# Two halves of the rows per partition, and an output in two pieces, in a row-wise Poisson loss kernel

## The chip, the core and the metric

The kernel runs on one core of one Trainium2 chip. The metric is the device time of one execution in microseconds (us), as a median over several runs. The profile is of one further execution, which has its own time and, within it, a span: the time from the first to the last instruction that the profiler recorded.

The core has a vector engine (DVE), a scalar engine (ACT), a general engine (POOL, GpSimd), a matrix engine (unused here) and a sync engine (SP). SP issues all of this kernel's memory transfers (DMAs), which run on 16 DMA engines between the chip's memory (HBM) and the on-chip memory of 128 partitions (SBUF). Engines wait for each other and for DMAs by semaphores; a finished DMA adds 16 to its semaphore.

## What is computed

```
batch, dim = 1024, 4096                       # float32
log_input = np.random.randn(batch, dim)
target    = np.random.randint(0, 10, (batch, dim)).astype(np.float32)

loss = np.exp(log_input) - target * log_input
return np.mean(loss, axis=-1).astype(np.float32)     # 1024 numbers
```

Two inputs of 16.8 MB each are read once, and 4 KB are written.

## The kernel before

Each of the 128 partitions takes 8 rows of the inputs, called rows 0 to 7 of the partition; a row is d = 4096 elements, 16 KB. In the kernel before, partition p has the rows 8p to 8p+7 of the batch, which lie behind one another in memory: 128 KB of each input per partition. Below, x is log_input and t is target.

**Loads (L62 to L69, issued at L123 to L133).** Thirteen loads alternate between x and t, all on SP, in this order: rows 0 to 3 of x, then of t (64 KB a partition, 8 MB each); rows 4 and 5 of x, then of t (32 KB a partition, 4 MB each); row 6 of x, then of t (16 KB a partition); and row 7 in the seven pieces of `TAIL` (in 32nds of a row: x 24, t 12, t 12, x 6, t 5, x 2, t 3). Every load covers all 128 partitions. The first four are moved ahead of the program's first barrier by `before_first_barrier`. Rows 6 and 7 reuse the buffers of rows 0 to 3 (`x_big`, `t_big`; see `place`), so the load of row 6 waits until the first exponential and the first product are done, and the loads of row 7 until four of each are (L124 to L127). Rows 4 and 5 have the buffers `x_mid` and `t_mid`. Each load has its own semaphore, `landed[i]`; the last of them, `landed[-1]`, belongs to the last piece of x, and the last load of all, the last piece of t, counts on `last_ready`.

**ACT (L149 to L166).** For each row of x, or piece of row 7, one activation computes the exponential, throws the values away (`e_dump`) and keeps the sum (`accum_out`). For rows 0 to 6 a small second activation (`join`, L139 to L147) later adds the row's sum of exponentials and DVE's sum of negated products, scales by 1/d, writes the result to column `row` of `all_loss` and raises `join_done`.

**DVE (L169 to L202).** For each row of t, or piece of row 7, one instruction multiplies t and x, and keeps the negated sum. The last one (L193) also multiplies the partial sums of row 7, which lie right behind the data, with a stretch of -1, and so closes row 7: it writes column 7 of `all_loss` and raises `loss_done`. It waits for the last load and for the last exponential.

**Output (L205 to L212).** SP waits for all seven joins and for `loss_done`, and writes `all_loss`, 128 partitions of 8 numbers, to the output in one DMA; then it clears the semaphores and waits for that DMA.

What decides where a row of the batch goes is three views of the inputs and the output (L57 to L59), and with them the distance in memory between the pieces that neighbouring partitions read in one load.

Of the kernel before, what the change touches and what calls it, by code (L numbers as in the profile page):

```python
# [30 lines left out]
def kernel(tc, log_input, target, out):  # L31
# [11 lines left out]

    nc = tc.nc
    tc.close()
    tc.compile()  # L48

    P = nc.NUM_PARTITIONS  # L50
    n, d = log_input.shape
    nb = n // P
# [1 line left out]
    inv_d = 1.0 / d  # L54
    last_row = nb - 1

    x_v = log_input.rearrange("(p b) d -> p (b d)", b=nb)  # L57
    t_v = target.rearrange("(p b) d -> p (b d)", b=nb)
    out_v = out.rearrange("(p b) -> p b", b=nb)  # L59


    loads = []  # L62
# [30 lines left out]
    def place(what, lo, w):  # L93
        row = lo // d
        if 4 <= row < 6:
            return mid[what][:, lo - 4 * d : lo - 4 * d + w]
        if row >= 6:
            lo -= (6 if row == 6 else 4) * d
        return big[what][:, lo : lo + w]
# [5 lines left out]
    all_loss = nc.alloc_sbuf_tensor("all_loss", [P, nb], F32).ap()  # L105
# [4 lines left out]
    landed = [nc.alloc_semaphore(f"landed{i}") for i in range(len(loads) - 1)]  # L110
# [5 lines left out]
    join_done = nc.alloc_semaphore("join_done")  # L116
    ones_done = nc.alloc_semaphore("ones_done")
    loss_done = nc.alloc_semaphore("loss_done")
    out_done = nc.alloc_semaphore("out_done")
# [3 lines left out]
    for i, (what, lo, w) in enumerate(loads):  # L123
        if what == "x" and lo in (6 * d, 7 * d):  # L124
            free = 1 if lo == 6 * d else 4
            nc.sync.wait_ge(exp_done, free)
            nc.sync.wait_ge(prod_done, free)  # L127
        src = x_v if what == "x" else t_v
        dma = nc.sync.dma_start(out=place(what, lo, w), in_=src[:, lo : lo + w])  # L129
        dma.then_inc(landed[i] if i < len(loads) - 1 else last_ready, 16)  # L130
        if lo < 6 * d:
            early.append(dma.ins)
# [16 lines left out]
    for k, (lo, w, i) in enumerate(x_work):  # L149
# [3 lines left out]
        elif col == 0 and row == 1:  # L153
            nc.scalar.wait_ge(exp_done, k)
        nc.scalar.activation(  # L155
            out=e_dump[:, col : col + w],
            in_=place("x", lo, w),
# [11 lines left out]
    for j, (lo, w, i) in enumerate(t_work):  # L169
# [4 lines left out]
        if j < n_t - 1:  # L174
            nc.vector.tensor_tensor_reduce(  # L175
                out=place("t", lo, w),
# [12 lines left out]
        else:  # L189
# [4 lines left out]
                out=place("t", lo, w + n_parts),  # L194
# [7 lines left out]
            ).wait_op(last_ready, 18, "sem-ge").then_inc(loss_done, 1)  # L202


    nc.sync.wait_ge(join_done, last_row)  # L205
    nc.sync.dma_start(out=out_v, in_=all_loss).wait_op(loss_done, 1, "sem-ge").then_inc(
        out_done, 16
    )
    used = landed + [last_ready, exp_done, prod_done, join_done, ones_done, loss_done]
    nc.sync.sem_clear(range(used[0].num, out_done.num))  # L210
    assert all(used[0].num <= s.num < out_done.num for s in used)
    nc.sync.wait_ge(out_done, 16).then_inc(out_done, -16)  # L212


# [28 lines left out]
```

## Time and profile before

| what | value |
|---|---|
| median of 7 runs | 84.04 us (83.95 to 84.72) |
| the profiled execution, its whole time | 84.15 us |
| its span | 82.8 us |
| DMA | 33.56 MB in 2016 packets, mean 405 GB/s |
| DVE busy | 35.6 us, 22 instructions |
| ACT busy | 33.2 us, 35 instructions |
| last piece of x landed | 80.20 us into the span |
| output's DMA issued | 81.36 us into the span |

A packet is one row of a load on one DMA engine (one partition's piece), or one of the 16 small writes that report a DMA's end: 14 DMAs of 128 rows and 16 reports make the 2016. The share of the DMA is the mean busy share of the 16 engines. In the chain of waits the profile follows the work that ended last back to what released each step; "issue" is time in which nothing shown was waited for, and SPq is an issue on SP. L129 and so on are lines of the kernel.

### The profile page before, as it was taken

What the parts mean: (1) busy time and instruction counts of PE and PEld (TensorE: products, weight loads), DVE (VectorE), ACT (ScalarE), POOL (GpSimd) and SP (SyncE); (2) the same over time, 40 slices, a digit from 0 to 9 for tenths busy, and PEclk for the clock granted to TensorE, in tenths of its full rate; (3) what the DMA queues carried; (4) which work ended last, traced back from release to release, by engine and by line L of the source; (5) the groups of instructions that cost most, each with busy time, mean ns of one, the idle gap of its engine ahead of it and who ended that gap; (6) DMA issues with size and microseconds to landing.
All of it is one profiled execution on the core that took longest, in us unless ns stands there. A gap on an engine that the chain in (4) does not pass through costs nothing.

```text
span 82.8 us, 131 instructions
## 1 busy us (share of the span) xinstructions
DVE 35.6 (43%) x22; ACT 33.2 (40%) x35; POOL 0.3 (0%) x5
## 2 busy tenths in 40 slices
DVE  0000000000000000000199999999369995994992
ACT  0500000000499910000000998979792496019360
POOL 0000000000000000000000000000000000000000
DMA  9389999958999995899599799899899999999950
GB/s 507 158 348 507 507 507 507 443 222 348 507 507 507 507 443 222 348 507 507 253 507 475 301 491 491 364 412 507 348 404 404 467 396 433 392 421 427 408 205 2
DMA packets 2016, 33.56 MB, mean 405 GB/s; under 512 B 352, under 2 KB 608, under 8 KB 1120
## 3 DMA queue, kind: packets, MB, share of 16 engines
q1 hardware_dynamic: 2016, 33.56, 95.6%
HBM read 33.55 MB, written 0.00 MB: 405 GB/s over the span
## 4 chain that ended last, share of the span: by engine, by line
DMA 72%; DVE 18%; issue 4%; SPq 3%; ACT 1%
DMA t_big<-in_target_dram 49%; DMA x_big<-in_log_input_dram 23%; DVE t_big L175 17%; SPq L129 3%; DVE t_big L193 1%; ACT e_dump L155 1%; DVE parts L175 0%; SPq L127 0%; DVE all_loss L193 0%
## 5 line engine op out<-in xcount | busy, mean ns | idle before, releaser
L175 DVE CUSTOM_DVE_ANT_0 t_big<-t_big,x_big 128x4096 f32<-128x4096 f32 (+2 forms) x8 | 26.2, 3307 | 43.6 <-DMA t_big<-in_target_dram 43.4
L155 ACT ACTIVATE e_dump<-x_big 128x4096 f32<-128x4096 f32 (+3 forms) x8 | 21.8, 2729 | 24.1 <-DMA x_big<-in_log_input_dram 24.0
L175 DVE CUSTOM_DVE_ANT_0 t_mid<-t_mid,x_mid 128x4096 f32<-128x4096 f32 x2 | 8.8, 4424 | 2.1 <-DMA t_mid<-in_target_dram 2.1
L141 ACT ACTIVATE join_dump<-parts 128x2 f32<-128x2 f32 x7 | 1.4, 204 | 20.4 <-DVE parts L175 20.2
L155 ACT ACTIVATE e_dump<-x_mid 128x4096 f32<-128x4096 f32 x2 | 7.1, 3568 | 0.0
L155 ACT ACT_TABLE_LOAD x1 | 1.3, 1283 | 3.0 <-PEq L48 3.0
L155 ACT ACTIVATION_READ_ACCUMULATOR e_dump<-x_big 128x1 f32 x8 | 1.5, 186 | 0.0
L141 ACT ACTIVATION_READ_ACCUMULATOR join_dump<-parts 128x1 f32 x7 | 1.3, 187 | 0.0
L193 DVE CUSTOM_DVE_ANT_0 t_big<-t_big,x_big 128x390 f32<-128x390 f32 x1 | 0.6, 566 | 0.1
L175 DVE DVE_READ_ACCUMULATOR2_ANT parts<- 128x1 f32 x7 | 0.6, 84 | 0.0
L155 ACT ACTIVATION_READ_ACCUMULATOR e_dump<-x_mid 128x1 f32 x2 | 0.4, 186 | 0.0
L175 DVE DVE_READ_ACCUMULATOR2_ANT t_big<- 128x1 f32 x3 | 0.2, 82 | 0.0
L136 POOL MEMSET x_big<- 128x6 f32 x1 | 0.1, 104 | 2.6 <-POOLq L48 2.6
L227 POOL MEMSET const-uint8-127<- 128x1 uint8 x1 | 0.1, 103 | 0.0
L227 POOL MEMSET const-bfloat16-1.0<- 128x1 bf16 x1 | 0.1, 102 | 0.0
L227 POOL MEMSET const-float32-0.0<- 128x1 f32 x1 | 0.1, 99 | 0.2 <-issue 0.2
L227 POOL MEMSET const-float32-1.0<- 128x1 f32 x1 | 0.1, 99 | 0.0
L193 DVE DVE_READ_ACCUMULATOR2_ANT all_loss<- 128x1 f32 x1 | 0.1, 84 | 0.0
## 6 DMA issues: line engine op xcount, KB each, us to landing
x_mid<-in_log_input_dram SPq DMA_DIRECT2D x1, 4096.0 KB, 50.0
t_mid<-in_target_dram SPq DMA_DIRECT2D x1, 4096.0 KB, 59.3
x_big<-in_log_input_dram SPq DMA_DIRECT2D x1, 2048.0 KB, 20.0
t_big<-in_target_dram SPq DMA_DIRECT2D x1, 2048.0 KB, 24.5
x_big<-in_log_input_dram SPq DMA_DIRECT2D x1, 1536.0 KB, 15.5
t_big<-in_target_dram SPq DMA_DIRECT2D x2, 768.0 KB, 17.7
x_big<-in_log_input_dram SPq DMA_DIRECT2D x1, 384.0 KB, 18.9
t_big<-in_target_dram SPq DMA_DIRECT2D x1, 320.0 KB, 19.2
```

Source lines behind the costliest of these rows:

```text
L129: dma = nc.sync.dma_start(out=place(what, lo, w), in_=src[:, lo : lo + w])
L136: nc.gpsimd.memset(big["x"][:, 4 * d : 4 * d + n_parts], -1.0).then_inc(ones_done, 1)
L141: nc.scalar.activation(out=join_dump[:, 2 * row : 2 * row + 2], in_=parts[:, 2 * row : 2 * row + 2], func=ACT_F.Copy, scale=inv_d, accum_o ...
L155: nc.scalar.activation(out=e_dump[:, col : col + w], in_=place("x", lo, w), func=ACT_F.Exp, bias=0.0, scale=1.0, accum_out=parts[:, 2 * ro ...
L175: nc.vector.tensor_tensor_reduce(out=place("t", lo, w), in0=place("t", lo, w), in1=place("x", lo, w), scale=-1.0, scalar=0.0, op0=ALU.mult ...
L193: nc.vector.tensor_tensor_reduce(out=place("t", lo, w + n_parts), in0=place("t", lo, w + n_parts), in1=place("x", lo, w + n_parts), scale= ...
L227: nc = _bacc.Bacc("TRN2", target_bir_lowering=False, num_devices=1)
```

## The change

The batch is cut into two halves of 512 rows. Partition p now has the rows 4p to 4p+3 of the first half as its rows 0 to 3, and the rows 4p to 4p+3 of the second half (512+4p and on) as its rows 4 to 7. The list of loads, their sizes, their order and waits stay; the pieces of neighbouring partitions in one load are 64 KB apart in memory instead of 128 KB. The first load of x and the first load of t each read 8 MB that lie without a gap; rows 4 and 5 together, row 6, and the pieces of row 7 are read with gaps, in stretches of 32 KB, 16 KB and less, 64 KB apart.

The output belongs to two separate places for each partition, and is written by two DMAs of 128 partitions of 4 numbers. The first is issued once the last piece of x has landed and the joins of rows 0 to 3 are done, the second when the rest is done. The wait at the end is for both.

```diff
-    x_v = log_input.rearrange("(p b) d -> p (b d)", b=nb)
-    t_v = target.rearrange("(p b) d -> p (b d)", b=nb)
-    out_v = out.rearrange("(p b) -> p b", b=nb)
+    x_v = log_input.rearrange("(h p b) d -> p h (b d)", h=2, p=P)
+    t_v = target.rearrange("(h p b) d -> p h (b d)", h=2, p=P)
+    out_v = out.rearrange("(h p b) -> p h b", h=2, p=P)
+    half = nb // 2
...
-        dma = nc.sync.dma_start(out=place(what, lo, w), in_=src[:, lo : lo + w])
+        h, at_lo = divmod(lo, half * d)
+        dma = nc.sync.dma_start(out=place(what, lo, w), in_=src[:, h, at_lo : at_lo + w])
...
+    nc.sync.wait_ge(landed[-1], 16)
+    nc.sync.dma_start(out=out_v[:, 0, :], in_=all_loss[:, :half]).wait_op(
+        join_done, half, "sem-ge"
+    ).then_inc(out_done, 16)
     nc.sync.wait_ge(join_done, last_row)
-    nc.sync.dma_start(out=out_v, in_=all_loss).wait_op(loss_done, 1, "sem-ge").then_inc(
-        out_done, 16
-    )
+    nc.sync.dma_start(out=out_v[:, 1, :], in_=all_loss[:, half:]).wait_op(
+        loss_done, 1, "sem-ge"
+    ).then_inc(out_done, 16)
...
-    nc.sync.wait_ge(out_done, 16).then_inc(out_done, -16)
+    nc.sync.wait_ge(out_done, 32).then_inc(out_done, -32)
```

In the changed kernel the loads are issued at L132, the first output at L209 and the second at L213.

## The prediction

> **What bounds the kernel now.** I read the page's queue part and the shares of the chain first, because they name the resource that is short.
>
> ```profile
> DVE 35.6 (43%) x22; ACT 33.2 (40%) x35; POOL 0.3 (0%) x5
> ...
> q1 hardware_dynamic: 2016, 33.56, 95.6%
> ...
> DMA 72%; DVE 18%; issue 4%; SPq 3%; ACT 1%
> ```
>
> The one DMA queue is busy for 95.6% of sixteen engines' span, and no compute engine is busy for half of it. The 18% that the chain gives to DVE is work done while the transfers run on (the chain follows a buffer that L127 waits for, at 58.7 us, and DMA is busy all that while).
>
> Then I asked for the DMA share and rate by window (last two columns), to see whether the transfers run at a ceiling of the engines or lose time between packets or in memory.
>
> ```profile
> 1.00:1.50 0.50, 0.00 (x0) 0.00 (x0) 0.00 (x0) 1.00 6.15 2097
> ...
> 6.00:7.00 1.00, 0.00 (x0) 0.00 (x0) 0.00 (x0) 1.00 2.42 1049
> 41.00:59.00 18.00, 17.47 (x8) 12.01 (x15) 0.00 (x0) 1.00 1.01 433
> 59.00:73.00 14.00, 11.22 (x5) 7.87 (x8) 0.00 (x0) 1.00 0.96 408
> 73.00:80.50 7.50, 6.18 (x7) 4.37 (x7) 0.00 (x0) 1.00 0.91 366
> ...
> 82.00:82.50 0.50, 0.00 (x0) 0.00 (x0) 0.00 (x0) 1.00 0.15 8
> ```
>
> A packet counts in the window in which it starts, so a short window can show a share over 1. 2097 GB/s for 0.5 us is 1.05 MB, sixteen packets of 64 KB, one for each engine; their share, 6.15 x 0.5 us, is 3.07 us a packet. From 6 to 7 us another sixteen start and take 2.42 us each. So the first packets are 0.65 us longer than the later ones, and a later one moves at 65,536 B / 2.42 us = 27.1 GB/s, or 433 GB/s for sixteen. From 41 to 59 us the measured rate is that same 433 with a share of 1.01: no engine idles. At 433 GB/s the 33.55 MB need 77.5 us; they take some 79.0 (first packets from about 1.1 us, the last data at about 80.2). The missing 1.5 us are the 0.65 of the first packets and the small packets of the tail (366 GB/s after 73 us).
>
> Last I read the end of the chain, for what follows the last byte, and SP's timeline, because the new instruction stands on SP.
>
> ```profile
> 61.14 19.06 DMA x_big<-in_log_input_dram
> 80.20 0.02 issue
> 80.22 0.52 ACT e_dump L155 x2
> 80.74 0.02 issue
> 80.76 0.57 DVE t_big L193
> 81.33 0.01 DVE all_loss L193
> ```
>
> ```profile
> 58.74 0.33 SPq L129 DMA_DIRECT2D x_big<-in_log_input_dram  x1
> 59.11 0.98 SPq L129 DMA_DIRECT2D t_big<-in_target_dram  x2
> 60.13 0.44 SPq L129 DMA_DIRECT2D x_big<-in_log_input_dram  x1
> 60.61 0.48 SPq L129 DMA_DIRECT2D t_big<-in_target_dram  x1
> 61.14 0.46 SPq L129 DMA_DIRECT2D x_big<-in_log_input_dram  x1
> 61.64 0.44 SPq L129 DMA_DIRECT2D t_big<-in_target_dram  x1
> 81.36 0.35 SPq L206 DMA_DIRECT2D out_dram<-all_loss  x1
> ```
>
> ```profile
> out_dram<-all_loss SPq DMA_DIRECT2D x1, 4.0 KB, 1.4
> ```
>
> After the last piece of x lands (80.20) come the last exponential, the closing DVE reduction, the output's issue at 81.36, and its landing 1.4 us later (82.76), which is the end of the 82.8 us span. The profiled execution took 84.15, so 1.35 lie around the span; the median of the seven runs is 84.04, 0.11 below. I sum against 84.15 and take the 0.11 off at the end.
>
> **The change, part by part.** *Where the loads read from.* All thirteen loads keep 128 partitions, bytes per partition, order and waits; only the distance in memory from one partition's piece to the next falls from 128 KB to 64 KB, so that the two 8 MB loads read one unbroken stretch and the others read half or less of a stretch with gaps. Packets are no larger. In the steady part a packet takes what sixteen busy engines give it (2.42 us, 433 GB/s at full share), whether it belongs to the 8 MB loads (64 KB packets) or to the 4 MB loads between 41 and 59 us (32 KB pieces, 128 KB apart, half of memory skipped): skipping costs nothing there. So I price the steady part at 0. The cover for that is the engines' own rate: were it memory that set the 2.42 us, each 1% of packet time would be worth 0.79 us.
>
> The only place where the trace leaves room for the address is the first sixteen packets, 0.65 us over the rest. Either that is the cost of starting (nothing is in flight before), which no layout changes, or sixteen engines that start together at equal distances meet in the same part of memory, which another distance may cure or make worse. Bounds: -0.65, the excess gone, and +0.65, as much again. The trace has no second cold start to decide by. I take 0: the loads that begin later, at other addresses and with the queue full, show no such excess (the 41 to 59 us window holds the starts of 4 MB loads and is at the ceiling), which fits a cost of starting.
>
> The Trainium skill has a rule here, in "DMA: Bandwidth & Descriptors", section "Latency and other measured facts": HBM-to-HBM copies whose rows lie a large power of two apart slow down, 207 GB/s at 512 KiB and 103 at 4 MiB against 214 in full, and tensors should be laid out contiguously. By that rule the change goes the good way, but its mildest entry loses 3%, already at four times our distance, and the 433 GB/s windows leave nothing of the kind at 128 KB; by the rule at its mildest the sum would be 3% of 79 us lower, some 81.7, an estimate that the rows contradict.
>
> *The early output.* One DMA of 128 rows of 16 B (columns 0 to 3 of all_loss) is issued after landed[-1], the semaphore of the last x piece, and after four joins. The joins of rows 0 to 3 are over by 60 us, so landed[-1] decides: 80.20. SP then issues from about 80.25 to 80.6 (0.35, the row at 81.36), and the data land 1.4 us after the issue's start, about 81.65. Queued behind it on SP are the wait for seven joins (the last at 77.5 us) and the final output, which needs loss_done at 81.34. So SP is free 0.7 us before it is wanted. No load stands behind it: L129's last issue is at 61.64. Nobody but the final wait looks for this output's landing, 1.1 us before the final one. Cost on the path: 0. What hides it is the 1.14 us of exponential and reduction; if that cover were gone, the price is one more issue, 0.44 to 0.48 by the rows that follow one another.
>
> The Trainium skill speaks against such a split, in "DMA: Bandwidth & Descriptors", section "Rules for kernel authors": many small transfers should be coalesced into one, since below 64 KB nearly all is overhead. Put on the path in full, the row's 1.4 us would give 84.04 + 1.4 = 85.4; the trace puts it beside the last exponential and reduction.
>
> *The final output.* 2 KB instead of 4 KB, still 128 rows. In the window from 82.0 to 82.5 us the output's 128 packets and 16 completion writes share 0.15 x 0.5 us x 16 = 1.2 us, 8.3 ns each, nine on an engine: 0.075 us in all. Half the bytes can save at most half of that, 0.04; the rows give no sign that a 16 B packet is quicker than a 32 B one, so 0. Its issue is 0.35 after long idleness and 0.43 to 0.49 right behind another; here some 0.75 us of idleness lie between, nearer to the first: 0, with +0.14 as the bound. Four instead of two rows of results now share 64 B of memory; if that slowed the writes, the nearest row is again the 0.075 us, so +0.08 when doubled. The final wait for 32 instead of 16 is the same instruction: 0.
>
> *The compute engines.* Same instructions, sizes and order on DVE, ACT and GpSimd; only which rows of the inputs they work on differs. 0.
>
> Sum: 84.15 + 0 = 84.15 for a profiled execution, or 84.04 for the median; I write 84.05. The forecast's own bounds: -0.04 for the smaller output, +0.22 for the issue and the small writes, and 0.1 either way, from the six runs that lie between 83.95 and 84.10: 83.9 to 84.35.
>
> **The rivals.** *A: the start was a collision, and the denser layout cures it.* For: sixteen packets at 3.07 against 2.42 us, and all loads gain a shorter distance. Against: the excess looks like a cold start. Price: up to -0.65, so 83.4; it decides from 0.42 on.
>
> *B: the denser layout collides.* Sixteen engines in step at half the distance lose what the first packets lost once more, at the start or where a load begins. For: the same excess. Against: full rate in the windows. Price +0.65: 84.7, slower; it decides when the extra packet time passes 0.42 us on the slowest engine, 17% of one 64 KB packet.
>
> *C: the early output gets into the way of the final one.* If SP or the queue takes longer than 1.1 us over the first (its landing takes 1.4), the second starts late: +0.44 to +0.48, so 84.5. Against: six issues in a row, 0.5 us apart at most.
>
> *D: the change doesn't do what it says.* If the loads were cut into other packets, their count would change. The instructions have the same shapes; I expect 2016 + 128 + 16 = 2160 packets. Under D the time is 84.04 too.
>
> **How the numbers follow.** Differences below about 0.5% (0.42 us) can't be told from none here. Forecast, with D: 0.73. A: 0.13. B: 0.08. C: 0.06. Thus faster 0.13, same 0.73, slower 0.14. The range takes in the forecast's own 83.9 to 84.35, the weaker half of A and C, and most of the way to B: 83.55 to 84.6.
>
> **What would show it.** Right: the 41 to 59 us rate stays at 433; the first sixteen packets stay near 3.07 us; the last x piece lands at 80.0 to 80.4; L209 issues right there and L213 about 1.1 us later, landing after 1.4. A shows as a shorter first share (under 5.5), B as a longer one or a lower rate in a window, C as L213 issued more than 0.1 us after loss_done. A steady rate over 433 would prove wrong that the engines set the pace, and with it the forecast.

## The result: slower by 0.9%, and the profile after

The changed kernel takes 84.86 us in the median of 12 runs (84.51 to 85.3), the kernel before 84.04 in 31 runs. The ratio is 1.0094, 95% interval 1.0072 to 1.0116: slower by 0.6 to 1.0 us, clear of the 0.5% named above. The single runs are spread over 0.8 us; of the 31 of before, 27 lie between 83.83 and 84.19. The profiled execution, 84.67 us with a span of 83.3, is one of the shorter ones; against that of before (84.15, 82.8) it is 0.5 us longer.

The page first: packets and busy share of the DMA queue of the changed kernel, and the line of the output DMAs (count, KB each, median us from issue to landing).

```profile
q1 hardware_dynamic: 2160, 33.56, 95.2%
```

```profile
out_dram<-all_loss SPq DMA_DIRECT2D x2, 2.0 KB, 2.0
```

There are 144 packets more, as one more DMA of 128 rows makes, so the loads are cut as before. The output's two DMAs land 2.0 us after their issue in the middle of the two; the one DMA of before took 1.4.

The windows of the changed kernel (busy time of DVE, ACT and POOL, clock, then DMA share and GB/s) show the load stream.

```profile
1.00:1.50 0.50, 0.00 (x0) 0.00 (x0) 0.00 (x0) 1.00 5.61 1835
...
6.00:7.00 1.00, 0.00 (x0) 0.00 (x0) 0.00 (x0) 1.00 2.27 983
41.00:59.00 18.00, 17.47 (x8) 11.95 (x15) 0.00 (x0) 1.00 1.01 435
59.00:73.00 14.00, 11.33 (x5) 7.94 (x9) 0.00 (x0) 1.00 0.96 398
73.00:80.50 7.50, 5.98 (x7) 4.29 (x7) 0.00 (x0) 1.00 0.94 379
```

1835 GB/s for 0.5 us is fourteen packets of 64 KB, and their share makes 5.61 x 0.5 x 16 / 14 = 3.2 us each; fifteen start from 6 to 7 us and take 2.42 us each (2.27 x 16 / 15). From 41 to 59 us the rate is 435 GB/s at full share. All this is as before: a slower first packet, then the same ceiling.

The end of its chain, and SP's issues in its timeline:

```profile
61.14 19.14 DMA x_big<-in_log_input_dram
80.28 0.02 issue
80.30 0.52 ACT e_dump L158 x2
80.82 0.02 issue
80.84 0.57 DVE t_big L196
81.41 0.01 DVE all_loss L196
```

```profile
80.35 0.35 SPq L209 DMA_DIRECT2D out_dram<-all_loss  x1
...
81.44 0.34 SPq L213 DMA_DIRECT2D out_dram<-all_loss  x1
```

The last x piece lands 0.08 us later than in the profile of before, and the final output is issued 0.08 later (81.44 against 81.36), 0.02 after loss_done, as before. Up to there 0.08 of the 0.5 us are explained. The rest lies after the issue. By the view of one line, L209 and L213 (us from the issue to the landing):

```profile
L209 SPq DMA_DIRECT2D out_dram<-all_loss x1: 348/348/348, 80.3 to 80.3; - x1
...
DMA to landing us min/median/max: 2.2/2.2/2.2
```

```profile
L213 SPq DMA_DIRECT2D out_dram<-all_loss x1: 344/344/344, 81.4 to 81.4; - x1
...
DMA to landing us min/median/max: 1.9/1.9/1.9
```

1.4 us have become 1.9 for the final output, and 2.2 for the early one, which had nothing behind it on SP for 0.7 us. Both report to one semaphore, sixteen reports each, one for each DMA engine; the view takes the 16th report as the landing of the first and the 32nd as that of the second. When each report arrived is in the trace too (us into the span):

```
before   packets 82.20-82.39   16 reports: 82.61 to 82.77
changed  packets 81.19-81.38   11 reports: 81.60 to 81.68, then 82.13 82.14 82.59 82.59 82.60
         packets 82.28-82.47   16 reports: 82.69 to 83.30
```

The packets go out as before, in 0.19 us. What is late is the report that the writes have arrived: eleven engines of the first output report 0.2 to 0.3 us after its last packet, the other five 0.7 to 1.2 us after it. So the question for the runs was why a 2 KB write with nothing to do but land is slow, and why it matters.

### The profile page after: what moved, and what is told of

Its sections match the earlier page's. It is cut to its first block, busy times and chain, and to the rows that moved or that the text cites. A ratio compares the mean times of both kernels' runs of the same rounds, so it can differ in the third digit from the quotient of the medians.

```text
span 83.3 us, 133 instructions
## 1 busy us (share of the span) xinstructions
DVE 35.6 (43%) x22; ACT 33.2 (40%) x35; POOL 0.3 (0%) x5
## 2 busy tenths in 40 slices
DMA packets 2160, 33.56 MB, mean 403 GB/s; under 512 B 496, under 2 KB 752, under 8 KB 1264
## 3 DMA queue, kind: packets, MB, share of 16 engines
q1 hardware_dynamic: 2160, 33.56, 95.2%
## 4 chain that ended last, share of the span: by engine, by line
DMA 72%; DVE 18%; issue 4%; SPq 3%; ACT 1%
DMA t_big<-in_target_dram 49%; DMA x_big<-in_log_input_dram 23%; DVE t_big L178 17%; SPq L132 3%; DVE t_big L196 1%; ACT e_dump L158 1%; DVE parts L178 0%; SPq L129 0%; DVE all_loss L196 0%
```

## The experiments

Each kernel ran in five rounds beside the kernel before on the same chip. "Landing" is the view above, of the profiled execution; where there are two outputs, the first one's stands first.

| run | what is written, and when | median us | ratio to before, 95% interval | landing us |
|---|---|---|---|---|
| changed kernel | 16 B rows, 1st half early, 2nd late | 84.86 | 1.0094, 1.0072 to 1.0116 | 2.2; 1.9 |
| e1 | new loads, 32 B rows, late | 84.03 | 1.0004, 0.9986 to 1.0023 | 1.4 |
| e2 | old loads, outputs as changed | 84.70 | 1.0081, 1.0057 to 1.0105 | 2.3; 2.0 |
| e3 | 2nd half alone, late | 84.10 | 1.0014, 1.0002 to 1.0025 | 1.4 |
| e4 | 1st half amid the loads, 2nd late | 85.30 | 1.0151, 1.0118 to 1.0183 | 16.7 with loads ahead of it; 1.4 |
| e5 | 1st half alone, early | 84.00 | 0.9993, 0.9972 to 1.0013 | 2.5 |
| e6 | both halves late | 86.07 | 1.0230, 1.0190 to 1.0271 | 1.8; 2.9 |
| e7 | two pieces of 32 B rows, early and late | 84.26 | 1.0023, 1.0008 to 1.0039 | 1.7; 1.6 |
| e8 | 32 B rows, early | 82.86 | 0.9859, 0.9830 to 0.9888 | 1.4 |
| e9 | 1st half alone, late | 85.32 | 1.0141, 1.0119 to 1.0163 | 2.3 |
| e10 | 2nd half alone, early | 83.01 | 0.9878, 0.9863 to 0.9894 | 1.4 |
| e11 | 16 B rows 32 B apart, early | 83.48 | 0.9934, 0.9912 to 0.9956 | 1.9 |
| e12 | 16 B rows 32 B apart, early and late | 84.09 | 0.9998, 0.9978 to 1.0018 | 1.8; 1.4 |
| e13 | as e9, read from columns 4 to 7 | 85.05 | 1.0135, 1.0113 to 1.0158 | 2.3 |
| e14 | as e3, read from columns 0 to 3 | 84.16 | 1.0025, 1.0015 to 1.0036 | 1.4 |
| e15 | changed, both read from offset 16 | 84.88 | 1.0106, 1.0087 to 1.0124 | 2.4; 2.1 |
| e16 | as e3, read from offset 32 | 84.21 | 1.0028, 1.0008 to 1.0047 | 1.4 |
| e17 | as e13, 1 KB further on | 85.49 | 1.0171, 1.0158 to 1.0185 | 2.7 |
| e18 | as e13, into another tensor | 84.25 | 1.0026, 1.0010 to 1.0042 | 1.4 |

Where nothing is written after loss_done (e5, e8, e10, e11), the time is not that of a whole kernel: the final output is missing.

### The two halves of the change apart: e1 and e2

e1 has the changed kernel's loads and the output of before:

```diff
-    out_v = out.rearrange("(h p b) -> p h b", h=2, p=P)
+    out_v = out.rearrange("(p b) -> p b", b=nb)
...
-    nc.sync.wait_ge(landed[-1], 16)
-    nc.sync.dma_start(out=out_v[:, 0, :], in_=all_loss[:, :half]).wait_op(
...
+    nc.sync.dma_start(out=out_v, in_=all_loss).wait_op(loss_done, 1, "sem-ge").then_inc(
...
```

> The loads of the changed kernel, the single output DMA of the kernel before (128 rows of 32 B after loss_done); so the 1024 results stand in another order than the reference's. Theory W (writes: the time is lost in the landing of the 16 B output rows, which took 1.9 us against 1.4 in the two profiles): 84.0 to 84.15, the output lands 1.4 us after its issue. Theory L (layout: the loads at 64 KB distance end later, by the 0.08 us of the profile or more in other executions): 84.5 to 84.9.

e2 has the loads of before and the changed kernel's outputs:

```diff
-    out_v = out.rearrange("(p b) -> p b", b=nb)
+    out_v = out.rearrange("(h p b) -> p h b", h=2, p=P)
+    half = nb // 2
...
+    nc.sync.wait_ge(landed[-1], 16)
+    nc.sync.dma_start(out=out_v[:, 0, :], in_=all_loss[:, :half]).wait_op(
+        join_done, half, "sem-ge"
+    ).then_inc(out_done, 16)
     nc.sync.wait_ge(join_done, last_row)
...
+    nc.sync.dma_start(out=out_v[:, 1, :], in_=all_loss[:, half:]).wait_op(
...
```

> The loads of the kernel before, the two output DMAs of the changed kernel; so the results stand in another order than the reference's. Theory W: 84.7 to 84.95, the second output lands about 1.9 us after its issue, with the same spread from execution to execution as the changed kernel (84.5 to 85.3). Theory L: 84.0 to 84.15.

84.03 and 84.70 us. The layout of the loads is worth nothing either way (within 0.25%), and the two outputs carry all of the loss. Theory L is gone.

### Is a 16 B row slow, or the company of the other output? e3 and e4

e3 leaves the early output away:

```diff
-    nc.sync.wait_ge(landed[-1], 16)
-    nc.sync.dma_start(out=out_v[:, 0, :], in_=all_loss[:, :half]).wait_op(
-        join_done, half, "sem-ge"
-    ).then_inc(out_done, 16)
...
-    nc.sync.wait_ge(out_done, 32).then_inc(out_done, -32)
+    nc.sync.wait_ge(out_done, 16).then_inc(out_done, -16)
```

> The changed kernel without the first output DMA; the first 512 results are not written. Theory W1 (a write of 16 B rows is slow by itself): 84.6 to 84.95, landing 1.8 to 1.9 us. Theory W2 (the first output, still landing when the second is issued, holds the second up): 84.0 to 84.15, landing 1.4 us. Theory L: 84.5 to 84.9 with a landing of 1.4 us.

e4 moves it in front of the second load of row 7:

```diff
         if lo < 6 * d:
             early.append(dma.ins)
+        if what == "x" and lo == last_row * d:
+            nc.sync.dma_start(out=out_v[:, 0, :], in_=all_loss[:, :half]).wait_op(
+                join_done, half, "sem-ge"
+            ).then_inc(out_done, 16)
...
-    nc.sync.wait_ge(landed[-1], 16)
-    nc.sync.dma_start(out=out_v[:, 0, :], in_=all_loss[:, :half]).wait_op(
```

> The changed kernel with the first output DMA issued between the loads of row 7 (about 59.5 us), so that it is written in the middle of the stream and has landed long before the second. Theory W1: 84.7 to 85.1 (landing 1.9 us, and up to 0.1 us for 128 more packets in the stream). Theory W2: 84.0 to 84.25, landing 1.4 us.

e3: 84.10 us, and its line in the view of the DMA issues (KB, us to landing) reads

```profile
out_dram<-all_loss SPq DMA_DIRECT2D x1, 2.0 KB, 1.4
```

So the second output is not slow by itself: it is slow when the first one is still under way. That is W2, and the second output of e4, long after the first, bears it out with 1.4 us. But e4 as a whole took 85.30 where W2 expected 84.0 to 84.25. Its windows, and then those of the changed kernel, show where (last two columns: DMA share and GB/s):

```profile
73.00:74.00 1.00, 1.00 (x1) 0.00 (x0) 0.00 (x0) 1.00 0.89 340
74.00:75.00 1.00, 0.75 (x2) 0.00 (x0) 0.00 (x0) 1.00 1.22 369
75.00:76.00 1.00, 0.00 (x0) 0.71 (x1) 0.00 (x0) 1.00 0.81 338
76.00:77.00 1.00, 0.15 (x1) 1.00 (x1) 0.00 (x0) 1.00 1.08 347
77.00:78.00 1.00, 1.00 (x1) 1.00 (x2) 0.00 (x0) 1.00 0.90 344
```

```profile
73.00:74.00 1.00, 1.00 (x1) 0.00 (x0) 0.00 (x0) 1.00 0.95 399
74.00:75.00 1.00, 0.89 (x2) 0.65 (x1) 0.00 (x0) 1.00 1.00 418
75.00:76.00 1.00, 0.00 (x0) 1.00 (x1) 0.00 (x0) 1.00 1.03 430
76.00:77.00 1.00, 0.76 (x1) 1.00 (x1) 0.00 (x0) 1.00 1.02 430
77.00:78.00 1.00, 1.00 (x2) 0.50 (x4) 0.00 (x0) 1.00 0.97 393
```

In e4 these five microseconds carry 1.74 MB of loads instead of 2.07, 16% less, at nearly the same share: packets take longer. (From 66 to 73 us single windows of the changed kernel lie between 356 and 459 GB/s, so one window alone says little.) The small writes set out at 73.21 us, and their reports come from 73.73 to 75.74. The last x piece then lands at 80.82 us instead of 80.28, and everything behind it moves with it. The profiled execution, 84.78 us, is the fastest of the six runs of e4, so this accounts for 0.6 of the 1.3 us that the median is over before. So a small write can also hold up the loads around it; whether they meet in the engines or in the memory is not shown.

### Why is the first output slow? e5 to e8

e5 leaves the second output away (SP waits for loss_done in its place):

```diff
-    nc.sync.dma_start(out=out_v[:, 1, :], in_=all_loss[:, half:]).wait_op(
-        loss_done, 1, "sem-ge"
-    ).then_inc(out_done, 16)
+    nc.sync.wait_ge(loss_done, 1)
```

> The changed kernel without the second output DMA (the last 512 results are not written); SP still waits for loss_done. What lands is the first output, issued at 80.3 us with nothing behind it. Theory N (the two writes hinder each other, because the second follows within some 1.1 us): the first alone lands 1.4 us after its issue, at 81.7, and the time is that of loss_done, about 81.5 to 81.8 in the span, 82.8 to 83.2 in all. Theory R (a small write that comes so soon after the load stream is slow by itself, and then holds the next one up): it lands after 1.9 to 2.3 us, at 82.2 to 82.6, 83.5 to 83.9 in all.

e6 holds the first back:

```diff
-    nc.sync.wait_ge(landed[-1], 16)
+    nc.sync.wait_ge(join_done, last_row)
+    nc.sync.wait_ge(loss_done, 1)
     nc.sync.dma_start(out=out_v[:, 0, :], in_=all_loss[:, :half]).wait_op(
```

> The changed kernel with the first output DMA also held until loss_done, so that the two are issued one right behind the other, 0.4 us apart, a microsecond further from the loads. Theory N: they still hinder each other, 84.8 to 85.4. Theory R: both land 1.4 us after their issue; the second issue ends the kernel, 84.04 + 0.4 = 84.4 to 84.55.

e7 and e8 start from the kernel before, with a tile of zeros that GpSimd fills early on:

```diff
...
+    nc.sync.wait_ge(ones_done, 2)
+    nc.sync.dma_start(out=out_v[:64, :], in_=zeros[:64, :]).wait_op(
+        landed[-1], 16, "sem-ge"
+    ).then_inc(out_done, 16)
     nc.sync.wait_ge(join_done, last_row)
-    nc.sync.dma_start(out=out_v, in_=all_loss).wait_op(loss_done, 1, "sem-ge").then_inc(
+    nc.sync.dma_start(out=out_v[64:, :], in_=all_loss[64:, :]).wait_op(
+        loss_done, 1, "sem-ge"
...
```

> The loads of the kernel before; the output in two DMAs of 64 rows of 32 B, at the same two moments and to the same two halves of the output as in the changed kernel. The first sends zeros from a tile of its own, so the first 512 results are zero. Theory S (it is the 16 B rows: two DMAs are harmless when each row is 32 B): 84.0 to 84.2, landing 1.4 us. Theories N and R, if row size is no matter: 84.5 to 84.9, landing 1.8 us or more.

```diff
...
+    nc.sync.wait_ge(ones_done, 2)
+    nc.sync.dma_start(out=out_v, in_=zeros).wait_op(
+        landed[-1], 16, "sem-ge"
+    ).then_inc(out_done, 16)
     nc.sync.wait_ge(join_done, last_row)
-    nc.sync.dma_start(out=out_v, in_=all_loss).wait_op(loss_done, 1, "sem-ge").then_inc(
+    nc.sync.wait_ge(loss_done, 1)
```

> The loads of the kernel before; a single output DMA of 128 rows of 32 B, of zeros, issued when the last piece of x has landed; no results are written, SP still waits for loss_done. Theory N or S: lands 1.4 us after its issue, at 81.6 to 81.7, 82.8 to 83.2 in all. Theory R without regard to row size: lands after 1.9 to 2.3 us, 83.5 to 83.9 in all.

The issue lines of e5 and of e8:

```profile
out_dram<-all_loss SPq DMA_DIRECT2D x1, 2.0 KB, 2.5
```

```profile
out_dram<-zeros SPq DMA_DIRECT2D x1, 4.0 KB, 1.4
```

The first output is slow with nothing behind it, 2.5 us and even above R's 2.3, so N falls, at least as the cause. But 32 B rows at the same moment, to all of the output, are not slow, so nearness to the loads alone (R) is not the cause either; and two DMAs of 32 B rows to the same two halves cost 0.25 us, not 0.8. That figure lies above S's 84.0 to 84.2; the rows of e7 in SP's timeline show where:

```profile
80.00 0.53 SPq L208 DMA_DIRECT2D out_dram<-zeros  x1
81.15 0.47 SPq L212 DMA_DIRECT2D out_dram<-all_loss  x1
```

The issues took 0.53 and 0.47 us instead of 0.35, and the second's packets set out at 82.27, 1.12 us after the start of their issue instead of 0.84; why the issues are longer was not tried. The reports come within 0.17 us of one another in both DMAs, as in the kernel before. e6 is the worst of all, 86.07, beyond every theory's range: issued 0.4 us apart, the two outputs' reports go on until 84.79 us, 2.0 us after the second's first packet (82.81). So close together the reports cannot be told apart by their count, and the landings of e6 in the table are rough.

Until here the first and the second half had each been tried at one moment only. e3 had the second half late, e5 the first half early.

### Moment or place? e9 to e12

e9 and e10 exchange them (each has one output only):

```diff
...
-    nc.sync.dma_start(out=out_v[:, 1, :], in_=all_loss[:, half:]).wait_op(
+    nc.sync.dma_start(out=out_v[:, 0, :], in_=all_loss[:, :half]).wait_op(
         loss_done, 1, "sem-ge"
...
```

> The changed kernel with one output DMA only, late (after loss_done), which sends columns 0 to 3 to the first half of the output; the last 512 results are not written. Beside e3 (the second half, late, alone: landed in 1.4 us) and e5 (the first half, early, alone: 2.5 us). Theory T (the moment: 16 B rows are slow within some 1 us of the load stream): as e3, 84.0 to 84.15, landing 1.4 us. Theory P (the place: the first half of the output is written slowly whenever it is): landing 1.9 to 2.5 us, 84.5 to 85.1.

```diff
+    nc.sync.wait_ge(ones_done, 2)
     nc.sync.wait_ge(landed[-1], 16)
-    nc.sync.dma_start(out=out_v[:, 0, :], in_=all_loss[:, :half]).wait_op(
+    nc.sync.dma_start(out=out_v[:, 1, :], in_=zeros[:, half:]).wait_op(
         join_done, half, "sem-ge"
...
```

> The changed kernel with one output DMA only, early (when the last piece of x has landed), which sends four columns of zeros to the second half of the output; no results are written. Theory T: as e5, landing 1.9 to 2.5 us, 83.6 to 84.2. Theory P: landing 1.4 us, 82.8 to 83.2.

The issue lines of e9 and of e10:

```profile
out_dram<-all_loss SPq DMA_DIRECT2D x1, 2.0 KB, 2.3
```

```profile
out_dram<-zeros SPq DMA_DIRECT2D x1, 2.0 KB, 1.4
```

The first half is slow late as well (85.32 us, landing 2.3), the second half is not slow early (83.01, landing 1.4). Theory T falls, P stands: it is not when, but where.

e11 and e12 are made from the kernel before, and test whether rows of 16 B suffer from sharing 32 B with a neighbour:

```diff
+    nc.sync.wait_ge(landed[-1], 16)
+    nc.sync.dma_start(out=out_v[:, :4], in_=all_loss[:, :4]).wait_op(
+        join_done, 4, "sem-ge"
+    ).then_inc(out_done, 16)
     nc.sync.wait_ge(join_done, last_row)
-    nc.sync.dma_start(out=out_v, in_=all_loss).wait_op(loss_done, 1, "sem-ge").then_inc(
+    nc.sync.wait_ge(loss_done, 1)
```

> The loads of the kernel before; one output DMA only, early, of 16 B rows as in e5, but 32 B apart in memory (columns 0 to 3 of the output as it was, so each row has 32 B of memory for itself); half of the results are not written. Theory G (a row of 16 B is slow because its neighbour's write falls into the same 32 B): landing 1.4 us, 82.8 to 83.2. If 16 B alone is enough to be slow: landing 1.9 to 2.5 us, 83.6 to 84.2 as e5.

In e12 the last line is a second DMA, of columns 4 to 7, after loss_done.

> The loads and the order of results of the kernel before; the output in two DMAs, columns 0 to 3 early and columns 4 to 7 after loss_done, rows of 16 B that are 32 B apart in each. Nothing is left out. Theory G: within a DMA no two rows share 32 B, and 1.1 us lie between the two, so 84.0 to 84.2. If 16 B alone is enough: 84.6 to 85.0 as the changed kernel.

e11 came between: landing 1.9 us, 83.48 in all, 0.5 to 0.6 us more than e8 and e10 and 0.5 less than e5. G is not borne out: rows that share their 32 B with no other row of their DMA are still late on seven engines of sixteen. e12 nevertheless costs nothing, 84.09. The reports tell how the two go together:

```
e11  packets 81.25-81.43   9 reports: 81.65 to 81.71, then 7 from 81.99 to 82.30
e12  packets 81.27-81.46   9 reports: 81.68 to 81.74, then 7 from 82.10 to 82.27
     packets 82.37-82.55   16 reports: 82.77 to 82.94
```

e12's first output is slow too, but it is through at 82.27, 0.1 us before the second's first packet, and then the second lands in 1.4 us. In the changed kernel the sixteenth report came at 82.60, when the second's packets had been out for up to 0.3 us. So a slow early write need not cost anything: in e12 it is done in time. The second output of e4, at the changed kernel's own addresses and with the first long done, landed in 1.4 us too.

### The place read or the place written? e13 to e16

The slow DMA and the quick one differ in two places: columns 0 to 3 or 4 to 7 of all_loss in SBUF, first or second half of the output. e12's two DMAs, both all over the output, pointed at the source. e13 and e14 cross the two, each from e3:

```diff
-    nc.sync.dma_start(out=out_v[:, 1, :], in_=all_loss[:, half:]).wait_op(
+    nc.sync.dma_start(out=out_v[:, 0, :], in_=all_loss[:, half:]).wait_op(
```

> The changed kernel with one output DMA only, late, from columns 4 to 7 of all_loss to the first half of the output; the last 512 results are not written. Beside e9 (columns 0 to 3 to the first half, 85.32). Theory S (the source: 16 B rows read from offset 0 of a 32 B piece of SBUF are slow, from offset 16 not): 84.0 to 84.15, landing 1.4 us. Theory D (the destination: the first half of the output is slow): 84.9 to 85.5, landing 1.9 to 2.5 us.

```diff
-    nc.sync.dma_start(out=out_v[:, 1, :], in_=all_loss[:, half:]).wait_op(
+    nc.sync.dma_start(out=out_v[:, 1, :], in_=all_loss[:, :half]).wait_op(
```

> The changed kernel with one output DMA only, late, from columns 0 to 3 of all_loss to the second half of the output; the first 512 results are not written. Beside e3 (columns 4 to 7 to the second half, 84.1). Theory S: 84.9 to 85.5, landing 1.9 to 2.5 us. Theory D: 84.0 to 84.15, landing 1.4 us.

e15 is the whole changed kernel with both sources moved; e16 is e3 read from columns 8 to 11 (8 in the place of 12 below):

```diff
-    all_loss = nc.alloc_sbuf_tensor("all_loss", [P, nb], F32).ap()
+    all_loss = nc.alloc_sbuf_tensor("all_loss", [P, 2 * nb], F32).ap()
+    def place_of(row):
+        return row + 4 if row < half else row - half + 12
...
-            accum_out=all_loss[:, row : row + 1],
+            accum_out=all_loss[:, place_of(row) : place_of(row) + 1],
```

> The changed kernel with all_loss twice as wide: rows 0 to 3 have columns 4 to 7 and rows 4 to 7 columns 12 to 15, so that both output DMAs read from offset 16 of a 32 B piece. Nothing is left out. Theory S: 84.0 to 84.15, both landing in 1.4 us. Theory D: 84.6 to 85.2 as the changed kernel.

> As e3 (one output DMA, late, to the second half), but the four numbers stand in columns 8 to 11 of the wider all_loss, offset 32 bytes; the first 512 results are not written. Theory S, with 32 B as the unit: 84.9 to 85.5, as e9. Theory S, with 64 B as the unit (offset 32 is as good as 16), or theory D: 84.0 to 84.15.

e13's issue line, and e14's:

```profile
out_dram<-all_loss SPq DMA_DIRECT2D x1, 2.0 KB, 2.3
```

```profile
out_dram<-all_loss SPq DMA_DIRECT2D x1, 2.0 KB, 1.4
```

It is the destination. The first half of the output takes 85.05 us from columns 4 to 7 and 85.32 (e9) from columns 0 to 3; the second half takes 84.1 to 84.2 from three sources (e3, e14, e16). The source theory falls entirely, and with it e15 as a repair: 84.88, no different from the changed kernel.

### What is it about the first half? e17 and e18

Both are e13 with another destination:

```diff
-    nc.sync.dma_start(out=out_v[:, 1, :], in_=all_loss[:, half:]).wait_op(
+    mid_v = out[256:768].rearrange("(p b) -> p b", p=P)
+    nc.sync.dma_start(out=mid_v, in_=all_loss[:, half:]).wait_op(
```

> As e13 (one output DMA only, late, 128 rows of 16 B from columns 4 to 7 of all_loss), written to bytes 1024 to 3071 of the output; the results before and behind are not written. If the whole first half is slow, half of the rows are: 84.5 to 85.2, landing 1.6 to 2.3 us. If only its first 1 KB is: 84.05 to 84.25, landing 1.4 us. If only its second 1 KB is: as e13, 84.9 to 85.5.

```diff
+    scratch = nc.dram_tensor("scratch", (1024,), F32, kind="Internal").ap()
+    scratch_v = scratch.rearrange("(h p b) -> p h b", h=2, p=P)
...
-    nc.sync.dma_start(out=out_v[:, 1, :], in_=all_loss[:, half:]).wait_op(
+    nc.sync.dma_start(out=scratch_v[:, 0, :], in_=all_loss[:, half:]).wait_op(
```

> As e13, but written to the first 2 KB of another tensor in the chip's memory, which nobody reads; no results are written. If the first half of a tensor of this size is slow as such: as e13, 84.9 to 85.5, landing 1.9 to 2.5 us. If it hangs on the address that the output has: most likely 84.05 to 84.25, landing 1.4 us; a slow one would leave it open.

The issue lines of e17 and of e18, and the reports:

```profile
out_dram<-all_loss SPq DMA_DIRECT2D x1, 2.0 KB, 2.7
```

```profile
scratch<-all_loss SPq DMA_DIRECT2D x1, 2.0 KB, 1.4
```

```
e13  packets 82.19-82.38   11 reports: 82.60 to 82.68, then 5 from 83.15 to 83.68
e17  packets 82.26-82.45    5 reports: 82.67 to 82.72, then 11 from 83.07 to 84.13
e18  packets 82.05-82.24   16 reports: 82.46 to 82.63
```

The first half of another tensor is not slow (84.25), so it is not the first half of a tensor as such, but the addresses that this output has. Of the three stretches of 2 KB tried, bytes 1024 to 3071 are the slowest. The time fits the case in which only the second 1 KB is slow, since both e13 and e17 write it; but both write it with 64 rows, and in e17 eleven engines are late instead of five. That speaks against each row meeting or missing a slow spot for itself; the lateness would then depend on which addresses are written together, or spread from the slow writes to others. None of this was tried, and e17 ran on another chip than e13. e12 adds a limit: its second output also puts half of its rows into the first 2 KB of the output, in the 16 B pieces between those of its first, and none of its reports is late. So that stretch is not slow for every row of 16 B at every time; whether the other pieces are quick by themselves or because the first output had just written beside them was not tried. What in the memory makes it so stays open. The slow first half was seen on two chips (e5 and e9 on one, e13 on another) and the slow stretch of e17 on a third.

Of the variants that write all results, none is faster than the kernel before; e12 equals it.

## Why the prediction was wrong, step by step

**What bounds the kernel** was right: with the new layout alone the time is 84.03, the rate stays at 433 to 435 GB/s in the same window, and the loads' own distance in memory does not matter. With that, the price of 0 for the steady part and for the start held; rivals A and B, which lived on the slower first packets, did not come about (3.2 us each against 3.07, and no gain or loss in e1). D did not come about either: there are the 2160 packets that were expected if the loads are cut as before. One reading in that part is wrong without harm: before, the 4 MB loads take 32 KB of each 128 KB, so they skip three quarters of the memory and not half, and the rate is full all the same.

**The early output** is the step that failed: "Nobody but the final wait looks for this output's landing, 1.1 us before the final one. Cost on the path: 0." In the sum this term stands at 0; the runs put it at 0.7 us with the old loads (e2) and 0.8 in the changed kernel. The prediction had checked who waits for it in the program, and which issues are queued behind it on SP. All of that held: L209 issued at 80.35, L213 at 81.44, 0.02 after loss_done. Of the signs of being right only the last failed, the landing of L213 after 1.4 us. What it left out is what the two DMAs share behind SP: the same engines and the same memory. The first output's landing overlaps the second's packets, and then the second takes 1.9 us in the place of 1.4 (0.44 of the 0.5 us in the profile). The same final output without the first one costs 0.1 us over before (e3), in the place of 0.8.

The landing that makes the overlap was mis-sized in the same part. The prediction took 1.4 us for the landing of the early output, from the one row of before, a DMA of 32 B rows; for slower writes of small rows it allowed +0.08 us, and for the final output only: as much again as the 0.075 us that an engine spends on its packets. The packets were the wrong thing to double. They went out in the same 0.19 us in all; the reports that the writes had arrived took 0.9 to 1.1 us longer (landings of 2.3 to 2.5 in e5 and e9). With 1.4 the first output would have been through at 81.75, half a microsecond before the second's packets at 82.28; with 2.2 it was not.

Rival C, "gets into the way of the final one", had the right victim with the wrong place: it looked for a late issue on SP, which did not happen, and priced one more issue, 0.44 to 0.48. The 0.44 that the profile loses after the issue falls on that number by chance; the median's 0.82 is beyond it and beyond the range. Its chance of 0.06 was far too small for a thing the trace of before could not show: it held no two output DMAs and no 16 B row.

Of the two rules weighed there, the one from the Trainium skill against many small transfers ("DMA: Bandwidth & Descriptors", "Rules for kernel authors") had the right sign, though not through the overhead of one more transfer (it says "mostly overhead", less than the prediction's "nearly all"): e12 has as many transfers and costs nothing. Another section of that page, "Queues, rings and completion order", says that the increment of a DMA's semaphore lands only after every earlier write from that DMA engine. That is a way in which a second DMA's report can wait for the first one's writes, but the times of the reports show that it is not enough here. In no run did the first report of 128 rows come less than 0.39 us after their first packet, so the sixteen reports up to 82.60 us in the changed kernel are the first output's: all its writes had landed before the second's reports were due, from 82.67 on. Ten of these came late all the same, up to 83.30. In e2 the sixteenth report came at 82.23, the second's were due from 82.24 on, and the last came at 83.05. So the second output's own writes or reports were slow; their packets had gone out while the first's writes were still landing. How the two hinder one another stays open.

## What to carry to other kernels

- An early piece of an output was free here only where it had landed before the next piece set out (e12, at no cost; 0.8 us in the changed kernel), and it was not free amid the loads (e4, 1.3 us). Not the program's waits alone decide, but also what two DMAs share behind the queue; leave room for a landing that is much longer than the one in the profile, or keep one DMA.
- The price of a small DMA is not in its packets but in the reports behind them, and these can depend on row size and address: here, in DMAs with no other output under way, rows of 32 B landed in 1.4 to 1.7 us wherever they were tried, and rows of 16 B behind the loads in 1.4 to 2.7. When a layout change cuts the rows of an output, count that as part of its price.
- Before a layout is changed for the sake of memory, see whether the rate in the windows already equals what all engines busy can move; then there is nothing to win.

## What the runs showed of the hardware that was not expected

- 128 rows of 16 B to the same tensor: landing 1.4 us for its second 2 KB, 2.3 to 2.5 for its first, 2.7 for bytes 1024 to 3071, and 1.4 for the first 2 KB of another tensor. Rows 32 B apart took 1.8 to 1.9 (e11, the first of e12), and 1.4 for the pieces between them, written after them. From where in SBUF they are read made no difference (85.05 and 85.32 against 84.10, 84.16 and 84.21).
- The same small write amid the load stream took the stream from 393 to 430 GB/s down to 338 to 369 for five microseconds (e4), and ended the kernel 1.3 us later than before in the median, though it is 2 KB out of 33.6 MB.
- Two outputs of 16 B rows, issued 0.4 us apart, cost 2.0 us (e6), more than the 0.8 of the same two 1.1 us apart; the first alone at that late moment costs 1.2 (e9).
